# Sums of weight blocks and gated products on GpSimd, and another listing of the merged blocks, in a one-core encoder layer

## The chip, the cores and the metric

The kernel runs on 1 core of one Trainium2 chip. The metric is device time in microseconds (us) of one execution; of the kernel before, 3 runs gave 1290.79 to 1299.38 us with a median of 1297.6 us. One further execution was profiled: it took 1294.25 us. The core has five instruction queues that are named here as the profile names them: PE (TensorE, matmuls; PEld is its weight load), DVE (VectorE), ACT (ScalarE), POOL (GpSimd) and SP (SyncE, here a queue for DMAs). Each queue runs in order, and an instruction at its head waits on semaphores for what it needs.

## The reference

One layer on 512 tokens of width 2048, in float32. The three branches (forgetting attention, chunked attention with a relative bias, stick-breaking attention) have 4 heads of 128 each.

```python
hn = rmsnorm(x, norm_g)
proj = jnp.einsum('bsd,dc->bsc', hn, w_in)            # 2048 -> 12292 columns
br = proj[..., :QKVG_COLS].reshape(b, s, 3, 4, 512)   # q, k, v, gate path of each branch
f_logit = proj[..., QKVG_COLS:QKVG_COLS + N_HEADS] + b_f
gates = jax.nn.sigmoid(proj[..., QKVG_COLS + N_HEADS:] + b_gate).reshape(b, s, 3, 2048)
ya = forgetting_attention(qa, ka, va, f_logit)        # qa, ka, qb, kb are normalised first
yb = chunked_relpos_attention(qb, kb, vb)
yc = stick_breaking_attention(qc, kc, vc)
ys = jnp.stack([ya, yb, yc], axis=2) * jax.nn.silu(br[:, :, :, 3])
up = jnp.einsum('bsnw,nwd->bsnd', ys, w_up)           # 512 -> 2048 in each branch
merged = jnp.sum(gates * up, axis=2)
return x + jnp.einsum('bsd,de->bse', merged, w_out)
```

## The kernel before

**Products of three matmuls.** A float32 product is made from parts that PE multiplies at its faster rate. A block of weights, 128x1024, is loaded into a tile `raw`; ACT writes its rounded part to `wh` (L409), DVE the rest, `wl = raw - wh` (L419), both in `prep`. PE then multiplies the high part of the activations by `wh`, the low part by `wh` and the high part by `wl` (L277). One block of weights is a *unit* of the program; PE works through 405 units in a fixed order. There are 2 buffers for `wl` and 3 for `wh` (`LA = 2`), so that the `wl` of a unit can be written from the end of the unit two before it.

**Strassen tasks.** The input projection of two column groups, and the output projection in two halves, are 2x2 block products with 7 products in place of 8 (`Strassen`, `Product`): 11 tasks for the input and 2 for the output, of 28 units each. A unit of a task is product p of chunk c, with 12 matmuls; the order is p = 5, 1, 6, 7, 2, 3, 4 with c = 0 to 3 in each (`PLAIN`; the first output task has another order). Products 1, 2, 4 load a block, product 5 loads one and has a second added to it by a DMA of the POOL queue that accumulates (`add_up`, L320). The weights of products 6 and 3 are sums in place: `sum_up` adds the block of (1, c) to that of (5, c), which makes the weights of (6, c), and later the block of (2, c) to that, which makes those of (3, c). These 104 sums are the DVE instruction L630. After the first of the two, the block of (1, c) gets another accumulating DMA and becomes the weights of (7, c). There are 8 `raw` buffers.

**The end of the program.** After the input tasks come 24 units of the up projection in four groups g of 512 columns, three branches b each (`up_units`, order in `UPS`). For each block of 128 tokens, DVE multiplies the product by its gate (L1321) and, for b = 1 and 2, adds it to the sum of the branches (L1328, 32 instructions). The merged blocks must be turned before the output projection, which is done in two ways. Groups in `DRAMS` (0, 2 and 1) are turned in 32x32 squares by DVE (L1354, `folded`), stored, and read back with their squares in new places by four SP DMAs a block (L312, `back`, called by `turned_m`). Group 3 is turned by PE (L1385, `spun_m`), and ACT copies the result from PSUM (L1392). A turned block is tile `m`, and `arrived` lets the sums begin that make the operands of the output projection: `merged_a` (groups 0 and 1, first DVE step L1401) and `merged_b` (groups 2 and 3). On PE the input tasks, the up units and the output tasks follow one another without a break in the program.

**What sets the order.** A planner in Python (`Flow`) runs through all steps before the program is written. A step is a generator that yields what it waits for, and an engine with an estimated cost; of the steps that could go first on an engine, the one with the earliest start is written next, and of equals the one with the earliest due time, which is its ready time and its slack. The planner's times decide the order in each queue and nothing else; on the chip the queues run on semaphores. `turned_m` waits in the planner's time for the estimated landing and `MEXTRA` more; but `arrived` then lets `merged_a` or `merged_b` begin from `flow.fin`, the end of the instruction written last, and not from that landing:

```python
        ev = yield from back(m, md[g][:, :, blk(i)])
        yield Event(ev.t + MEXTRA)
        arrived(g, i, m)
...
            spawn(merged_a(k, m), 4.0, flow.fin)
```

Of the kernel before, what the change touches and what calls it, by code (L numbers as in the profile page):

```python
# [16 lines left out]
S = 512  # L17
# [8 lines left out]
UK = 8  # L26
# [11 lines left out]
PE, ACT, DVE, SP, POOL = 0, 1, 2, 3, 4  # L38
# [26 lines left out]
class Flow:  # L65
# [16 lines left out]
    def give(self, slots, n=1):  # L82
        slots.free += [self.fin] * n

    def spawn(self, gen, slack, ready=None):
        task = Task(gen, slack, self.now if ready is None else ready)
        self.tasks.append(task)
        self.advance(task)
# [81 lines left out]

def dve_us(n, x=1):
    return x * (0.1 + 0.00105 * n)


@with_exitstack
def hybrid_kernel(
# [12 lines left out]
    nc = tc.nc  # L189
# [17 lines left out]
    flow = Flow()  # L207
    spawn, set_, give = flow.spawn, flow.set, flow.give
# [3 lines left out]
    def t2(s, dt=F32):  # L212
        return tp.tile([P, S], dt, tag="t2", name=nm(s))
# [13 lines left out]
    def blk(i):  # L227
        return slice(i * P, (i + 1) * P)
# [3 lines left out]
    def two(ap):  # L232

        return ap.rearrange("p (h s) -> p h s", h=2)
# [20 lines left out]
    def split(hi, lo, src, n, ev=None, due=(), hi_ev=None):  # L255

        yield (ACT, act_us(n), *due)
        nc.scalar.activation(hi, src, AF.Copy)
        if hi_ev is not None:
            set_(hi_ev)  # L260
        yield (DVE, dve_us(n), *due)
        nc.vector.tensor_sub(lo, src, f(hi))  # L262
        if ev is not None:
            set_(ev)

    def minus(to, a, b):

        nc.vector.scalar_tensor_tensor(to, a, -1.0, b, op0=ALU.mult, op1=ALU.subtract)
# [38 lines left out]
    def back(to, src):  # L307

        n = src.shape[0] * 4
        for b in range(4):  # L310
            yield issue(0.54)
            nc.sync.dma_start(to[32 * b:32 * (b + 1), :].rearrange("p (n c) -> p n c", c=32),  # L312
                              src.rearrange("t (a r) c -> (t a) r c", r=32)[:, :, 32 * b:32 * (b + 1)]
                              .rearrange("n r c -> r n c"))
            ev = Event(landing(flow.fin, n * 4, 128) + PIECES)
        return ev
# [60 lines left out]
    def at(u, g, slack=5.0):  # L377
        side.setdefault(u, []).append((g, slack))
# [44 lines left out]
    def products(u, ps, kts, tbs, block, first=False, last=False, bank=None, done=None, outer=False, gate=None,  # L423
                 more=False):

        for group in [[tb] for tb in tbs] if outer else [tbs]:
            if bank is not None:
                for tb in group:
                    yield bank[0], 1
                    ps[tb] = bank[1]()  # L430
            if gate is not None:
                for tb in group:
                    yield gate(tb)
            for j, kt in enumerate(kts):
                for tb in group:
                    yield lambda: block(kt, tb) is not None
                    h, lo, ev = block(kt, tb)
                    yield ev
                    yield PE, mm_us(S, 2)
                    mm(ps[tb], h, u.hi[:, j, :], first and j == 0, more=more)  # L440
                    mm(ps[tb], lo, u.hi[:, j, :], more=more)
            yield u.ready
            for j, kt in enumerate(kts):
                for tb in group:
                    yield PE, mm_us(S)
                    mm(ps[tb], block(kt, tb)[0], u.lo[:, j, :], stop=last and j == len(kts) - 1, more=more)
            if last:
                for tb in group:
                    spawn(done(tb), 1.0, flow.fin)
# [142 lines left out]
    class Product(Unit):  # L592
# [31 lines left out]
        def sum_up(self):  # L624
            task, c = self.task, self.c
            own, after = (5, 6) if self.p == 1 else (6, 3)
            to = task.unit(own, c)
            yield to.ready
            yield DVE, dve_us(2 * S)
            nc.vector.tensor_add(to.raw, to.raw, self.raw)  # L630
            set_(task.unit(after, c).there)
            if self.p == 2:
                give(raws)
                return
            u = task.unit(7, c)
            u.raw = self.raw
            yield from self.more(Event(flow.fin), u)
# [670 lines left out]
    merged, merged_ev = {}, {}  # L1308

    def up_units(g, b):  # L1310
        n = (C, B, A)[b]
        ps = [None] * QB
        for tb in range(QB):
            sig_ev[n, g, tb] = Event()
            merged_ev[b, g, tb] = Event()

        def taken(tb):
            yield sig_ev[n, g, tb]
            t = sig[n, g, tb]
            yield DVE, dve_us(S)  # L1320
            nc.vector.tensor_mul(t, ps[tb], t)  # L1321
            give(accs)
            if b == 0:
                merged[g, tb] = t
            else:
                yield merged_ev[b - 1, g, tb]
                yield DVE, dve_us(S)
                nc.vector.tensor_add(merged[g, tb], merged[g, tb], t)  # L1328
                give(t2s)
            set_(merged_ev[b, g, tb])  # L1330

        def mms(i):
            def block(k, tb):
                y = b * NH + 2 * i + k
                return ys[y] and (*ys[y].block(tb), y_ev[y])

            def go(u):
                yield from products(u, ps, (0, 1), range(QB), block, i == 0, i == 1, None if i else (accs, acc),
                                    done=taken, outer=True)
            return go  # L1340

        return [Unit(mms(i), srcs=[w_up[g, b, i]]) for i in range(2)]
# [7 lines left out]
    def folded(g, tb):  # L1350
        yield merged_ev[NB - 1, g, tb]
        m = merged[g, tb]
        yield DVE, dve_us(S) + 0.07
        nc.vector.transpose(m, m)  # L1354
        if g not in md:
            md[g] = dp.tile([QB, P, S], F32, name=nm("md"))
        md_ev[g, tb].t = (yield from store(md[g][tb], m, 256, t2s)).t + LATER
# [3 lines left out]
    def turned_m(g, i):  # L1361
        for tb in range(QB):
            yield md_ev[g, tb]
        yield t2s, 1
        m = t2("m")
# [4 lines that stand above are left out]
    def arrived(g, i, m):  # L1370
        k = 4 * g + i
        if k < UK:
            kept_m[k] = m
            spawn(merged_a(k, m), 4.0, flow.fin)
        else:
            spawn(merged_b(k - UK, m), 3.0, flow.fin)

    def spun_m(g, i):
        for tb in range(QB):
# [18 lines left out]
    def merged_a(k, a):  # L1398

        yield DVE, dve_us(HS)  # L1400
        nc.vector.tensor_sub(a[:, RH], a[:, LH], a[:, RH])  # L1401
        yield xps, 1
        m1[k] = Parts("m1", [m1_ev[k]] * 2)
        yield from split(m1[k].hi, m1[k].lo, two(a), S, m1_ev[k])

    def merged_b(k, b):
        a = kept_m[k]
        yield m1_ev[k]
        yield t2s, 1
        t = t2("mt")  # L1410
        if k % 2 == 0:
            yield t2s, 1
            mus[k // 2] = t2("mu")
        u = mus[k // 2][:, RH if k % 2 else LH]
        q = DVE, dve_us(HS)
        yield q
        minus(t[:, LH], b[:, RH], a[:, RH])
        yield q
        minus(t[:, RH], t[:, LH], a[:, LH])
        give(t2s)  # L1420
        yield q
        minus(u, t[:, LH], b[:, LH])
        yield xps, 1
        ev = Event()
        m23[k] = Parts("m23", [ev, ev])
        yield from split(m23[k].hi, m23[k].lo, two(t), S, ev)
        give(t2s)
        if k % 2 == 0:
            yield xps, 1
            m4[k // 2] = Parts("m4")  # L1430
            set_(m4_ev[k // 2])
        yield xps, 1
        ev = Event()
        m2[k] = Parts("m2", [ev, ev])
        yield from split(m2[k].hi, m2[k].lo, two(b), S, ev)
        give(t2s)
        yield m4_ev[k // 2]
        h, lo, ev = m4[k // 2].half(k % 2)
        yield from split(h, lo, u, HS, ev)
        if k % 2:  # L1440
            give(t2s)

    for g, b in UPS:
# [5 lines left out]
        for i in range(QB):  # L1449
            if g in DRAMS:  # L1450
                at(len(units) - 1, lambda g=g, i=i: folded(g, i))
# [100 lines left out]
NR = 8  # L1552

UPS = [(0, 0), (0, 1), (2, 0), (2, 1), (0, 2), (2, 2)] + [(g, b) for g in (1, 3) for b in range(3)]
DRAMS = (0, 2, 1)
MLATE, MSKIP = 2.5, 1

EARLY = 0.5
# [4 lines left out]
HSLACK = 12.0  # L1563
ENDSLACK, ENDOFF = 3.0, 3
EARLYG = 1
MEXTRA = 8.0

_OUT = (QB, NQ, P, S)

# [45 lines left out]
```

## Time and profile before

| | |
|---|---|
| runs | 1290.79, 1297.6, 1299.38 us |
| profiled execution | 1294.25 us, of which the span from the first to the last instruction is 1292.5 us |
| granted TensorE clock, mean | 0.996 |
| busy share of the span: PE, PEld | 99%, 81% |
| DVE, ACT, POOL | 77%, 58%, 7% |
| DMA | 286.51 MB, mean 222 GB/s |

"Busy" is read for each engine by itself: the PE row is an upper figure, since matmuls overlap and their ends are modelled. A row of the time line gives start, duration, engine, line of the code, operation, output <- inputs, shape, number of instructions merged in the row, and in square brackets the idle time before it with what ended that. A row of groups has the number of instructions, their busy time, the mean of one in ns, and the idle time before them. Line numbers are those of the kernel before; those of the kernel after are 4 higher from L175 to the end of the planned program.

### The profile page before, as it was taken

Reading aid. Unit: us, or ns where it says so; the run is one execution under the profiler, and the core shown is the slowest. Engines: PE = TensorE matmul, PEld = TensorE weight load, DVE = VectorE, ACT = ScalarE, POOL = GpSimd, SP = SyncE. Lnnn points to the kernel's source line nnn. Section 1 sums busy time; section 2 is a strip of 40 time slices with the busy share of each in tenths; the row PEclk is TensorE's granted clock in tenths of the full one; section 3 lists DMA queues with packets and bytes.
Section 4 is the critical chain, followed back from the end, with each engine's and each line's share of the span. In section 5 each row is a group of like instructions: output and inputs, shape, how many; then the busy total and the mean of one; then the engine's idle time right before and its main releaser. Section 6 shows DMA issues by size and latency. Waiting matters only on the chain. (4 is left out here: it accounts for less than half of the span.)

```text
span 1292.5 us, 17358 instructions
## 1 busy us (share of the span) xinstructions
PE 1274.2 (99%) x5700; PEld 1050.2 (81%) x5700; DVE 999.5 (77%) x1402; ACT 752.2 (58%) x1239; POOL 91.7 (7%) x115
## 2 busy tenths in 40 slices
PE   9999999999999999999999999999999998989998
PEld 7788888888888888888888788887887786868887
DVE  6948896978969677686876878868788686898665
ACT  7836565645756567565575665755656532564442
POOL 0001010110101101011010110101100000010100
PEclk9999999999999999999999999999999999989999
DMA  9685899987889878897889978889889979946963
GB/s 356 207 206 123 216 235 215 265 200 209 222 201 281 191 218 228 199 272 196 222 223 208 271 183 220 230 192 287 189 217 342 286 228 211 265 94 224 238 169 129
DMA packets 269690, 286.51 MB, mean 222 GB/s; under 512 B 178320, under 2 KB 189072, under 8 KB 269600
## 3 DMA queue, kind: packets, MB, share of 16 engines
q1 hardware_dynamic: 252176, 226.42, 59.0%
q0 software_dynamic: 14976, 54.53, 22.6%
q10 hardware_dynamic: 2448, 4.46, 0.9%
q8 instruction: 45, 0.74, 0.2%
q14 instruction: 45, 0.37, 0.1%
HBM read 241.78 MB, written 43.56 MB: 221 GB/s over the span
## 5 line engine op out<-in xcount | busy, mean ns | idle before, releaser
L419 DVE TENSOR_TENSOR wl<-raw,wh 128x1024 fp32r<-128x1024 f32 (+1 forms) x405 | 492.5, 1217 | 215.5 <-PE acc L277 138.7
L409 ACT ACTIVATE wh<-raw 128x1024 fp32r<-128x1024 f32 (+1 forms) x404 | 426.0, 1056 | 359.8 <-PE acc L277 327.9
L277 PE MATMUL acc<-wh,x 128*128 128x512 f32 x1664 | 424.0, 390 | 0.1
L277 PEld LDWEIGHTS acc<-wh,x 128*128 128x128 f32 x1664 | 312.0, 188 | 68.4 <-issue 3.4
L277 PE MATMUL acc<-wh,t 128*128 128x512 f32 x1056 | 275.4, 390 | 2.4 <-ACT wh L409 2.4
L277 PEld LDWEIGHTS acc<-wh,t 128*128 128x128 f32 x1056 | 197.3, 188 | 43.2 <-ACT wh L409 3.3
L277 PE MATMUL acc<-wl,x 128*128 128x512 f32 x832 | 232.2, 389 | 0.1
L277 PEld LDWEIGHTS acc<-wl,x 128*128 128x128 f32 x832 | 155.8, 188 | 32.5 <-DVE wl L419 0.5
L277 PE MATMUL acc<-wl,t 128*128 128x512 f32 x528 | 154.6, 391 | 0.2
L320 POOL DMA_DIRECT2D raw<-in_w_col x88 | 76.1, 865 | 846.4 <-DMA raw<-in_w_col 136.7
L630 DVE TENSOR_TENSOR raw<-raw,raw 128x1024 f32<-128x1024 f32 x104 | 126.7, 1218 | 0.1
L277 PEld LDWEIGHTS acc<-wl,t 128*128 128x128 f32 x528 | 98.2, 188 | 21.5 <-DVE wl L419 2.0
L277 PE MATMUL acc<-wh,m 128*128 128x512 f32 x448 | 114.4, 389 | 0.0
L277 PE MATMUL acc<-wh,y 128*128 128x512 f32 x384 | 104.2, 393 | 0.0
L277 PEld LDWEIGHTS acc<-wh,m 128*128 128x128 f32 x448 | 84.0, 188 | 17.5
L277 PEld LDWEIGHTS acc<-wh,y 128*128 128x128 f32 x384 | 72.6, 189 | 15.1
L277 PE MATMUL acc<-wl,m 128*128 128x512 f32 x224 | 64.7, 395 | 5.7 <-DVE wl L419 5.7
L277 PE MATMUL acc<-wl,y 128*128 128x512 f32 x192 | 60.4, 394 | 4.2 <-DVE wl L419 4.2
L714 ACT ACTIVATE u<-acc 128x512 f32<-128x512 f32 x52 | 31.1, 599 | 41.4 <-PE acc L277 41.3
L277 PEld LDWEIGHTS acc<-wl,m 128*128 128x128 f32 x224 | 42.3, 190 | 15.1 <-DVE wl L419 6.5
L277 PEld LDWEIGHTS acc<-wl,y 128*128 128x128 f32 x192 | 36.4, 191 | 12.7 <-DVE wl L419 5.3
L1321 DVE TENSOR_TENSOR sg<-acc,sg 128x512 f32<-128x512 f32 x48 | 32.6, 685 | 7.2 <-ACT sg L1305 3.6
(155 smaller groups left out, 951.3 us busy)
## 6 DMA issues: line engine op xcount, KB each, us to landing
raw<-in_w_col SPq DMA_DIRECT2D x191, 512.0 KB, 5.0
raw<-in_w_col POOLq DMA_DIRECT2D x88, 512.0 KB, 8.2
raw<-in_w_out SPq DMA_DIRECT2D x32, 512.0 KB, 4.8
raw<-in_w_up SPq DMA_DIRECT2D x24, 512.0 KB, 4.9
sg<-gl SPq DMA_DIRECT2D x48, 256.0 KB, 5.2
gl<-u SPq DMA_DIRECT2D x44, 256.0 KB, 4.8
raw<-in_w_out POOLq DMA_DIRECT2D x16, 512.0 KB, 6.8
qkl<-qd SPq DMA_DIRECT2D x96, 64.0 KB, 4.0
```

Of the source, the lines that this page charges most:

```text
L277: nc.tensor.matmul(ps, w, x, start=start, stop=stop, skip_group_check=more)
L320: nc.gpsimd.dma_start(to, src, accum_op=ALU.add)
L409: nc.scalar.activation(u.hi, u.raw, AF.Copy)
L419: nc.vector.tensor_sub(u.lo, u.raw, f(u.hi))
L630: nc.vector.tensor_add(to.raw, to.raw, self.raw)
L714: nc.scalar.activation(t, w, AF.Copy)
L1321: nc.vector.tensor_mul(t, ps[tb], t)
```

## The change

There are three edits. The 104 sums of weight blocks and the 32 sums of gated products become GpSimd instructions, on the POOL queue, with a cost of 0.2 + 0.0022 n us in the planner. The steps on turned blocks are listed from the estimated landing (`flow.ready` at that point is the landing with `MEXTRA`), `MEXTRA` is 4.0 and not 8.0, and the slack of `merged_a` is 1.0 and not 4.0; that of `merged_b` stays 3.0. Group 1 leaves `DRAMS`, so that PE turns it as it does group 3.

```diff
+def pool_us(n, x=1):
+    return x * (0.2 + 0.0022 * n)
...
             to = task.unit(own, c)
             yield to.ready
-            yield DVE, dve_us(2 * S)
-            nc.vector.tensor_add(to.raw, to.raw, self.raw)
+            yield POOL, pool_us(2 * S)
+            nc.gpsimd.tensor_add(to.raw, to.raw, self.raw)
             set_(task.unit(after, c).there)
...
                 yield merged_ev[b - 1, g, tb]
-                yield DVE, dve_us(S)
-                nc.vector.tensor_add(merged[g, tb], merged[g, tb], t)
+                yield POOL, pool_us(S)
+                nc.gpsimd.tensor_add(merged[g, tb], merged[g, tb], t)
                 give(t2s)
...
         if k < UK:
             kept_m[k] = m
-            spawn(merged_a(k, m), 4.0, flow.fin)
+            spawn(merged_a(k, m), MAS, max(flow.ready, flow.fin))
         else:
-            spawn(merged_b(k - UK, m), 3.0, flow.fin)
+            spawn(merged_b(k - UK, m), MBS, max(flow.ready, flow.fin))
...
-DRAMS = (0, 2, 1)
+DRAMS = (0, 2)
...
-MEXTRA = 8.0
+MEXTRA = 4.0
+MAS = 1.0
+MBS = 3.0
```

Since the planner has other costs, nearly every queue has another order; PE runs the same matmuls in the same order of units, with the attention products at other places between them. Three places are shown.

The DVE queue at products 1 of the fifth input task, before; `wl_3980` is that of unit (1, 0), `wl_4001`, `wl_4029` and `wl_4052` are those of (1, 1) to (1, 3), `wl_4078` is that of (6, 0):

```order
L419 TENSOR_TENSOR wl_3980<-raw_3800,wh_3955 128x1024
L630 TENSOR_TENSOR raw_3666<-raw_3666,raw_3800 128x1024
L902 STREAM_TRANSPOSE w_3912<-w_3912 128x384
L419 TENSOR_TENSOR wl_4001<-raw_3837,wh_3979 128x1024
L630 TENSOR_TENSOR raw_3694<-raw_3694,raw_3837 128x1024
L419 TENSOR_TENSOR wl_4029<-raw_3857,wh_3998 128x1024
L630 TENSOR_TENSOR raw_3720<-raw_3720,raw_3857 128x1024
L902 STREAM_TRANSPOSE v_3463<-v_3463 128x384
L419 TENSOR_TENSOR wl_4052<-raw_3882,wh_4028 128x1024
L630 TENSOR_TENSOR raw_3765<-raw_3765,raw_3882 128x1024
L419 TENSOR_TENSOR wl_4078<-raw_3666,wh_4051 128x1024
```

The same units on the DVE queue of the kernel after:

```order
L423 TENSOR_TENSOR wl_3975<-raw_3803,wh_3955 128x1024
L906 STREAM_TRANSPOSE w_3899<-w_3899 128x384
L423 TENSOR_TENSOR wl_4006<-raw_3834,wh_3974 128x1024
L906 STREAM_TRANSPOSE w_3912<-w_3912 128x384
L423 TENSOR_TENSOR wl_4030<-raw_3855,wh_4003 128x1024
L906 STREAM_TRANSPOSE v_3469<-v_3469 128x384
L423 TENSOR_TENSOR wl_4054<-raw_3883,wh_4029 128x1024
L423 TENSOR_TENSOR wl_4078<-raw_3663,wh_4053 128x1024
```

And its POOL queue there, where the sums now stand among the accumulating DMAs:

```order
L634 TENSOR_TENSOR raw_3663<-raw_3663,raw_3803 128x1024
L634 TENSOR_TENSOR raw_3690<-raw_3690,raw_3834 128x1024
L324 DMA raw_3803<-in_w_col 128x1024
L324 DMA raw_3834<-in_w_col 128x1024
L634 TENSOR_TENSOR raw_3719<-raw_3719,raw_3855 128x1024
L634 TENSOR_TENSOR raw_3776<-raw_3776,raw_3883 128x1024
L324 DMA raw_3855<-in_w_col 128x1024
L324 DMA raw_3883<-in_w_col 128x1024
```

The sums have left DVE; each accumulating DMA stands behind the sum of its block, and the third and fourth sums stand behind two of the DMAs.

The DVE queue of the kernel before at the first turned blocks; `m_9567` to `m_9569` are blocks of group 0 that a DMA brings back, and `wl_9627` is that of the 16th of the 24 up units:

```order
L1321 TENSOR_TENSOR sg_9443<-acc_9562,sg_9443 128x512
L419 TENSOR_TENSOR wl_9627<-raw_9275,wh_9577 128x1024
L1401 TENSOR_TENSOR m_9567<-m_9567 128x256
L1401 TENSOR_TENSOR m_9568<-m_9568 128x256
L1401 TENSOR_TENSOR m_9569<-m_9569 128x256
L262 TENSOR_TENSOR m_1681_9665<-m_9567,m_1681_9665 128x2x256
L419 TENSOR_TENSOR wl_9681<-raw_9311,wh_9625 128x1024
```

The same steps in the kernel after, where `wl_9727` is that of the 18th up unit:

```order
L423 TENSOR_TENSOR wl_9630<-raw_9282,wh_9581 128x1024
L423 TENSOR_TENSOR wl_9677<-raw_9315,wh_9628 128x1024
L1325 TENSOR_TENSOR sg_9483<-acc_9629,sg_9483 128x512
L1325 TENSOR_TENSOR sg_9484<-acc_9645,sg_9484 128x512
L1325 TENSOR_TENSOR sg_9530<-acc_9656,sg_9530 128x512
L1325 TENSOR_TENSOR sg_9531<-acc_9665,sg_9531 128x512
L423 TENSOR_TENSOR wl_9727<-raw_9367,wh_9676 128x1024
L1405 TENSOR_TENSOR m_9558<-m_9558 128x256
L1405 TENSOR_TENSOR m_9559<-m_9559 128x256
L1405 TENSOR_TENSOR m_9560<-m_9560 128x256
```

The steps on the first turned blocks have moved two units down the queue, behind the `wl` of the 18th up unit instead of the 16th.

The PE queue of the kernel after inside the 19th up unit; `sg_9390` to `sg_9445` are the merged blocks of group 1, whose last part was multiplied in the 18th:

```order
L281 MATMUL acc_9850<-wl_9779,y_8426 128x512
L1389 MATMUL att_9866<-identf,sg_9390 128x128
L1389 MATMUL att_9866<-identf,sg_9417 128x128
L1389 MATMUL att_9866<-identf,sg_9437 128x128
L1389 MATMUL att_9866<-identf,sg_9445 128x128
L1389 MATMUL att_9875<-identf,sg_9390 128x128
L1389 MATMUL att_9875<-identf,sg_9417 128x128
```

These 16 transposes are new on PE; they wait for the sums that GpSimd now makes, and the transposes of group 3 do so too, at the second unit of the output projection.

## The prediction

> **What bounds the kernel now.** The page of the profile comes first, then the waits of PE.
>
> ```profile
> span 1292.5 us, 17358 instructions
> PE 1274.2 (99%) x5700; PEld 1050.2 (81%) x5700; DVE 999.5 (77%) x1402; ACT 752.2 (58%) x1239; POOL 91.7 (7%) x115
> PE acc L277 <- DVE wl L419: 9.9, 3, 5.7
> PE acc L277 <- ACT wh L409: 2.4, 2, 1.5
> ```
>
> PE is the bound: it does matmuls nearly all the time, and DVE, busy for 77%, matters only where PE waits for a `wl`. It does so three times, 9.9 us in all, and the time line has the three places, with what DVE did there:
>
> ```profile
> 1076.48 1.07 PE L277 MATMUL acc<-wh,y 128*128 128x512 f32 x4
> 1077.68 1.43 DVE L1401 TENSOR_TENSOR m<-m 128x256 f32<-128x256 f32 x3 [10.05 <-DMA m<-md]
> 1079.62 1.22 DVE L419 TENSOR_TENSOR wl<-raw,wh 128x1024 fp32r<-128x1024 f32 x1
> 1080.89 0.73 PE L277 MATMUL acc<-wl,y 128*128 128x512 f32 x2 [3.34 <-DVE wl L419]
> 1089.10 0.73 PE L277 MATMUL acc<-wl,y 128*128 128x512 f32 x2 [0.83 <-DVE wl L419]
> 1132.27 0.43 DVE L1401 TENSOR_TENSOR m<-m 128x256 f32<-128x256 f32 x1 [6.25 <-DMA m<-md]
> 1136.82 2.08 PE L277 MATMUL acc<-wl,m 128*128 128x512 f32 x4 [5.71 <-DVE wl L419]
> ```
>
> All three are one fault of order: the steps on turned blocks stand in the DVE queue before their data has come back, so that DVE stands still for 10.05 and 6.25 us with a `wl` queued behind. Two stages of the time line and two rows of the chain of waits give the price with the slower clock that follows each pause:
>
> ```profile
> 1076.00:1090.00 14.00, 9.83 (x35) 7.27 (x34) 12.14 (x19) 7.86 (x12) 0.86 (x1) 0.88 0.80 153
> 1129.00:1143.00 14.00, 8.29 (x39) 6.70 (x37) 10.70 (x16) 5.84 (x9) 0.00 (x0) 0.76 0.37 69
> 1142.30 0.88 PE att L1385 x8
> 1143.18 145.43 PE acc L277 x640
> ```
>
> An undisturbed matmul takes 145.43 / 640 = 0.227 us, eight transposes 0.88 us. The first stage has 35 matmuls, 7.9 us of its 14.0; the second 23 and 16 transposes, 5.2 + 1.8 = 7.0 of 14.0. So 6.1 + 7.0 = 13.1 us are lost there, at a granted clock of 0.88 and 0.76.
>
> **The change part by part.**
>
> *The listing and the third group* take that cause away. The steps on group 0 now stand two up units further down the queue (24 matmuls each, 5.45 us at 0.227), 10.9 us, against a wait of 10.05 us. The blocks of group 1, for which DVE waited 6.25 us, come from PE and ACT and no DMA. I take all 13.1 us as gained. PE pays 16 transposes more, 2 x 0.88 = 1.8 us; the 16 DMAs and 4 DVE transposes that go were hidden. Sum: -11.3 us. Bounds: nothing gained and 1.8 lost, if the blocks land 5 us later than before, and -13.1.
>
> *The sums of gated products.*
>
> ```profile
> L1328 DVE TENSOR_TENSOR sg<-sg,sg 128x512 f32<-128x512 f32 x32 | 22.0, 690 | 0.7
> L630 DVE TENSOR_TENSOR raw<-raw,raw 128x1024 f32<-128x1024 f32 x104 | 126.7, 1218 | 0.1
> ```
>
> DVE is rid of 22.0 us that lay beside 130 us of PE work: nothing by itself. A sum on GpSimd is longer, but each has a whole up unit (5.45 us for four) until it is needed, except before the transposes, which are a rival below.
>
> *The sums of weight blocks* decide. DVE gets 126.7 us back, which is worth nothing while PE is the bound. What they can cost is time of DVE's `wl`. No row has a GpSimd sum; the nearest are three selects at the start, one beside a DVE instruction with two inputs in SBUF:
>
> ```profile
> 1.26 0.28 POOL L351 TENSOR_SCALAR_AFFINE_SELECT identf<-tmpc 128x128 f32<-128x128 f32 x1
> 1.50 0.28 POOL L354 TENSOR_SCALAR_AFFINE_SELECT mskc<-tmpc 128x128 f32<-128x128 f32 x1
> 5.02 0.74 DVE L491 SCALAR_TENSOR_TENSOR x<-x,small_in,x 128x512 fp32r<-128x512 f32 x1
> 5.22 0.70 POOL L468 TENSOR_SCALAR_AFFINE_SELECT mskf<-tmpc 128x128 f32<-128x128 f32 x1 [3.44 <-PE att L467]
> 6.11 0.75 DVE L491 SCALAR_TENSOR_TENSOR x<-x,small_in,x 128x512 fp32r<-128x512 f32 x1 [0.34 <-ACT x L486]
> ```
>
> For the price of a sum: 128 elements in 0.28 us make 8 x 0.28 = 2.24 us for 1024. That is one input. With two it could be twice that, 4.5 us; the lower bound is DVE's own 1.22. I take 2.25. For who waits: the third select took 0.70 and ended at 5.92, 0.16 after the DVE instruction, which took 0.74, no longer than the next of its kind, 0.75. So GpSimd was held up by DVE's two-input instruction. Whether a GpSimd instruction that is first holds up DVE, no row shows; I take it that it does, for its whole length.
>
> The Trainium skill says so ("SBUF — State Buffer", Who interferes with whom): a DVE instruction with two SBUF inputs and a GpSimd instruction that reads SBUF exclude each other, the first one keeping the shared port until it ends; here the trace agrees for DVE first. By the selects alone, DVE would lose nothing and the sum would end at -11.3 us; by the rule it pays what follows.
>
> The units at which it happens, in the fifth input task, DVE and PE:
>
> ```profile
> 432.31 1.22 DVE L419 TENSOR_TENSOR wl<-raw,wh 128x1024 fp32r<-128x1024 f32 x1
> 433.45 1.22 DVE L630 TENSOR_TENSOR raw<-raw,raw 128x1024 f32<-128x1024 f32 x1
> 435.03 1.23 DVE L419 TENSOR_TENSOR wl<-raw,wh 128x1024 fp32r<-128x1024 f32 x1 [0.36 <-issue]
> 437.80 1.19 DVE L419 TENSOR_TENSOR wl<-raw,wh 128x1024 fp32r<-128x1024 f32 x1
> 440.47 1.23 DVE L419 TENSOR_TENSOR wl<-raw,wh 128x1024 fp32r<-128x1024 f32 x1 [0.34 <-issue]
> 439.31 1.07 PE L277 MATMUL acc<-wl,x 128*128 128x512 f32 x4
> 441.12 0.62 PE L277 MATMUL acc<-wl,x 128*128 128x512 f32 x2
> 443.84 0.62 PE L277 MATMUL acc<-wl,t 128*128 128x512 f32 x2
> L320 POOL DMA_DIRECT2D raw<-in_w_col x88 | 76.1, 865 | 846.4 <-DMA raw<-in_w_col 136.7 <-DVE u L1162 126.0 <-DVE w L902 109.7
> ```
>
> The `wl` of (1, 1) starts at 432.31, those of (1, 2), (1, 3) and (6, 0) at 435.03, 437.80 and 440.47; PE uses the last three at 439.31, 441.12 and 443.84. A `wl` that starts on time so has 3.05, 2.13 and 2.14 us to spare. GpSimd's first two sums need nothing of these units and run before; the next two stand behind two DMAs, of which the second must wait until the `wl` of (1, 1) has read its block, at 433.53, and takes 0.87. The third sum runs from 434.4 to 436.7, and the `wl` due at 435.03 waits until then and ends at 437.9. If DVE and GpSimd take turns, the fourth sum then runs to 440.2, and the `wl` of (1, 3) to 441.4, where PE wants it at 441.1: 0.3 us of pause. If GpSimd does both sums in a row, to 438.9, the first `wl` ends at 440.1 for 439.31: 0.8 us. I take 0.6.
>
> At products 2 the blocks come from SP:
>
> ```profile
> 452.60 8.48 SPq L293 DMA_DIRECT2D raw<-in_w_col  x4
> ```
>
> Three steps in 8.48 us less one issue: they come at the pace of PE's units, 12 x 0.227 = 2.72 us, since a buffer comes free with each. Each turn of a sum and a `wl` is 2.25 + 1.22 = 3.47. After four turns DVE is up to 4 x 0.75 = 3.0 us late, or 0.9 beyond the 2.13 of the shortest unit, and where attention products lie between, as here, it is not late at all. I take 0.5.
>
> Behind the sums on POOL stand the accumulating DMAs, and behind those of products 2 the buffers that SP loads for products 4:
>
> ```profile
> raw<-in_w_col SPq DMA_DIRECT2D x191, 512.0 KB, 5.0
> raw<-in_w_col POOLq DMA_DIRECT2D x88, 512.0 KB, 8.2
> ```
>
> Both are hidden by units: (7, c) comes 8 units, 21.8 us, after (1, c), against 2.25 + 8.2; (4, c) 8 units after (2, c), against 2.25 + 5.0. A sum that is held up for 10 us would end that cover.
>
> So 1.1 us a task, for 11 input tasks and both output tasks (whose first takes its products 1 in pairs, so count 1.5): 12.5 x 1.1 = 13.8 us. A sum's 0.1 us more is 0.2 to 0.4 us in each of the two places, about 7 us in all.
>
> PE's other waits, 2.4 us for a `wh`, lie in input tasks where the planner has moved attention products and DMAs; I leave them as they are. **Sum**: 1294.25 - 11.3 + 13.8 = 1296.8 for an execution like the profiled one, which lay 3.35 below the median of the runs, 1297.6. So 1300 us, and 1292 to 1311 with a pause of 0.5 to 2.0 us a task.
>
> **The rivals.**
>
> *GpSimd never holds up DVE.* For it: the selects show only the reverse, and the sums have time (4 units of 2.72 us between (1, c) and (6, c)), so that a GpSimd that always gives way is early enough. Against it: a port that one side can hold is more simply held by either. Then 1297.6 - 11.3 = 1286 us, and 1283 if those 2.4 us go as well.
>
> *The sums are longer, and PE waits twice a task.* The mechanism is the one above, at the same units. With 2.6 us a sum, the third runs from 434.4 to 437.0 and the fourth at once to 439.6; the `wl` of (1, 2) ends at 440.8 for 439.31, 1.5 us; at products 2 four turns of 3.82 leave 4.4 late, 2.3 beyond. That is 3.8 a task, 47 us, and a net of +36: 1333 us; with turns taken, 0.9 at the first place and half of the 2.3 at the second, 2.1 a task, 26 us and 1312. It is over 1% slower from (13 + 11.3) / 12.5 = 1.9 us a task on, at sums of about 2.4 us. For it: two inputs are read where the select reads one. Against it: a fixed part of the 0.28 us, which does not grow.
>
> The Trainium skill gives 4497 ns for a GpSimd sum of 2048 float32 elements ("GPSIMD Engine Reference", Performance versus the Vector engine); half of that, 2.25 us, is an estimate by that page, and the sum by it is the 1300 above. No run here has shown it.
>
> *PE's transposes wait for GpSimd.* Those of group 3 stand 2.72 us behind the last up matmul: a DVE product, 0.69, and a sum, half of 2.25, leave 0.9 us for two hand-overs. If a `wl` of 1.22 comes between, PE pauses for under a microsecond at two places: 1302 us. If the order at the end does not heal, 11 us come back on top: 1313.
>
> **How the numbers follow.** Forecast, turns taken at about 2.25 us a sum: 0.38, of which little is above 1%. DVE never held up: 0.32, a quarter of it below -1%. Longer sums: 0.24, nearly all slower by over 1%. The end: 0.06, half of it slower. Faster by over 1% (under 1284.6; a run differs from the next by up to 0.7%, so 1% is about what can be told): 0.08. Slower by over 1% (over 1310.6): 0.22 + 0.03 + 0.03 of the forecast's edge = 0.28. Within: 0.64. The range reaches from the first rival to the middle of the second: 1283 to 1326. The likeliest time is 1300.
>
> **What would show it.** The groups of the profile after would have the sums on POOL at 2.2 to 2.3 us (a mean near 3 means that they wait for DVE), and the `wl` group with a mean well above 1217 ns if DVE is held up, 1217 if not; the waits would have PE waiting for `wl` at (1, 2), (1, 3), (6, 0) and at (3, 0) of most tasks, some 25 places. No DVE wait for `m<-md` over 2 us, and a clock near 1.0 between 1057 and 1143 us, would show the gain. A `wl` mean of 1217 with pauses of PE elsewhere would make the mechanism wrong; PE waiting for `wh` at (6, c) would say that GpSimd, not DVE, is late.

## The result and the profile after

The change made the kernel slower. Four runs gave 1399.1 to 1407.48 us with a median of 1403.65, beside 1294.19 for the kernel before on the same chip: a ratio of 1.0852, with a 95% interval of 1.0822 to 1.0882. The prediction said 1300 us, with a range up to 1326, and gave "slower by over 1%" a chance of 0.28. Direction and size were both missed.

The page of the profile after, with its first lines, the groups of the instructions in question, and PE's share of the waits; the last row is the group of `wl` in the profile before:

```profile
span 1400.2 us, 17458 instructions
PE 1314.3 (94%) x5716; PEld 1065.3 (76%) x5716; DVE 1060.1 (76%) x1262; ACT 755.4 (54%) x1243; POOL 429.2 (31%) x251
L423 DVE TENSOR_TENSOR wl<-raw,wh 128x1024 fp32r<-128x1024 f32 (+1 forms) x405 | 619.8, 1535 | 258.8 <-PE acc L281 180.7
L634 POOL TENSOR_TENSOR raw<-raw,raw 128x1024 f32<-128x1024 f32 x104 | 293.0, 2852 | 317.0 <-DMA raw<-in_w_col 231.4
L1332 POOL TENSOR_TENSOR sg<-sg,sg 128x512 f32<-128x512 f32 x32 | 50.1, 1577 | 113.9 <-DVE sg L1325 110.9
...
PEld acc L281 <- DVE wl L423: 46.7, 39, 3.3
PE acc L281 <- DVE wl L423: 30.0, 25, 2.9
PE att L278 <- DVE qkl L926: 13.3, 6, 4.7
PE att L1117 <- DVE al L266: 13.3, 11, 3.3
...
L419 DVE TENSOR_TENSOR wl<-raw,wh 128x1024 fp32r<-128x1024 f32 (+1 forms) x405 | 492.5, 1217 | 215.5 <-PE acc L277 138.7
```

DVE has 140 instructions fewer than before, and its busy time has risen, from 999.5 to 1060.1 us: the 405 steps that write `wl` take 1535 ns in the mean, where they took 1217. PE, busy for 99% before, is busy for 94% and waits for `wl` and for two DVE steps of the attention, `qkl` and `al`.

The loss isn't at the end of the program. Two stages of the time line from 17 to 1080 us, after and then before. In the kernel after they hold the input projection; the kernel before is through with it at 986 us and does up units behind that (in each row the stretch, its length, busy time and count of PE, PEld, DVE, ACT and POOL, the granted clock, the DMA share and GB/s):

```profile
17.00:400.00 383.00, 363.13 (x1578) 292.93 (x1577) 308.61 (x395) 217.37 (x361) 103.27 (x60) 0.98 0.77 201
400.00:1080.00 680.00, 633.14 (x2742) 514.49 (x2741) 513.73 (x608) 387.24 (x678) 208.38 (x116) 0.98 0.80 204
```

```profile
17.00:400.00 383.00, 382.94 (x1723) 314.67 (x1722) 308.48 (x450) 235.87 (x386) 27.74 (x32) 1.00 0.83 218
400.00:1080.00 680.00, 674.28 (x3018) 557.84 (x3016) 517.06 (x726) 407.75 (x711) 48.35 (x56) 1.00 0.86 232
```

In the same 1063 us PE does 4320 matmuls where it did 4741. The 421 that are missing are 96 us at 0.227 us each. Worked out from the records of PE, the 11 input tasks took 887.8 us before and take 986.3 us after, so that 98.5 us of the loss lie in them.

What one sum does to DVE and PE shows at products 1 of the fourth input task. DVE, POOL and PE on the time line:

```profile
377.14 1.18 DVE L423 TENSOR_TENSOR wl<-raw,wh 128x1024 fp32r<-128x1024 f32 x1
378.56 0.58 DVE L906 STREAM_TRANSPOSE w<-w 128x384 f32<-128x384 f32 x1 [0.24 <-ACT w L891]
379.44 6.26 DVE L423 TENSOR_TENSOR wl<-raw,wh 128x1024 fp32r<-128x1024 f32 x1 [0.30 <-PE acc L281]
379.56 5.04 POOL L634 TENSOR_TENSOR raw<-raw,raw 128x1024 f32<-128x1024 f32 x2
386.57 4.12 DVE L423 TENSOR_TENSOR wl<-raw,wh 128x1024 fp32r<-128x1024 f32 x1
386.93 2.67 POOL L634 TENSOR_TENSOR raw<-raw,raw 128x1024 f32<-128x1024 f32 x1
381.96 1.98 PE L281 MATMUL acc<-wh,x 128*128 128x512 f32 x8
385.75 1.56 PE L281 MATMUL acc<-wl,x 128*128 128x512 f32 x4 [1.82 <-DVE wl L423]
387.11 3.27 PE L281 MATMUL acc<-wh,x 128*128 128x512 f32 x8
390.75 1.19 PE L281 MATMUL acc<-wl,x 128*128 128x512 f32 x4 [0.38 <-DVE wl L423]
```

The `wl` that starts at 379.44 does its 1.2 us of work only when both sums are through, at 384.60, and ends at 385.70. GpSimd takes two sums in a row while DVE stands there, and the `wl` had started 0.12 us before the first of them. PE pauses for 1.82 us, and the eight matmuls behind, 1.98 us at 381.96, take 3.27 at 387.11: a slow clock follows the pause (0.65 granted in the mean from 387 to 391 us, 1.00 from 380 to 384). At 386.57 the same happens again with one sum.

### The profile page after: what moved, and what is told of

Read it like the earlier page. It is cut to its first block, busy times and chain, and to the rows that moved or that the text cites. A ratio compares the mean times of both kernels' runs of the same rounds, so it can differ in the third digit from the quotient of the medians.

```text
span 1400.2 us, 17458 instructions
## 1 busy us (share of the span) xinstructions
PE 1314.3 (94%) x5716; PEld 1065.3 (76%) x5716; DVE 1060.1 (76%) x1262; ACT 755.4 (54%) x1243; POOL 429.2 (31%) x251
## 5 line engine op out<-in xcount | busy, mean ns | idle before, releaser
L423 DVE TENSOR_TENSOR wl<-raw,wh 128x1024 fp32r<-128x1024 f32 (+1 forms) x405 | 619.8, 1535 | 258.8 <-PE acc L281 180.7
L281 PE MATMUL acc<-wh,x 128*128 128x512 f32 x1664 | 431.1, 395 | 5.0 <-ACT wh L413 4.5
L634 POOL TENSOR_TENSOR raw<-raw,raw 128x1024 f32<-128x1024 f32 x104 | 293.0, 2852 | 317.0 <-DMA raw<-in_w_col 231.4
L281 PE MATMUL acc<-wh,t 128*128 128x512 f32 x1056 | 278.4, 393 | 2.8 <-ACT u L718 2.8
L281 PE MATMUL acc<-wl,x 128*128 128x512 f32 x832 | 238.4, 397 | 23.2 <-DVE wl L423 22.7
L281 PE MATMUL acc<-wl,t 128*128 128x512 f32 x528 | 157.6, 396 | 0.8 <-DVE wl L423 0.7
L1332 POOL TENSOR_TENSOR sg<-sg,sg 128x512 f32<-128x512 f32 x32 | 50.1, 1577 | 113.9 <-DVE sg L1325 110.9
```

Of the source, the lines that this page charges most:

```text
L281: nc.tensor.matmul(ps, w, x, start=start, stop=stop, skip_group_check=more)
L423: nc.vector.tensor_sub(u.lo, u.raw, f(u.hi))
L634: nc.gpsimd.tensor_add(to.raw, to.raw, self.raw)
L1332: nc.gpsimd.tensor_add(merged[g, tb], merged[g, tb], t)
```

## The experiments

Of each kernel I give the median, the median of the kernel before on the same chip, and the ratio with its 95% interval. The diffs are against the kernel after, if nothing else is said.

**Both kinds of sums back on VectorE.** What is left of the change is the new listing and the third group on TensorE.

```diff
-            yield POOL, pool_us(2 * S)
-            nc.gpsimd.tensor_add(to.raw, to.raw, self.raw)
+            yield DVE, dve_us(2 * S)
+            nc.vector.tensor_add(to.raw, to.raw, self.raw)
...
-                yield POOL, pool_us(S)
-                nc.gpsimd.tensor_add(merged[g, tb], merged[g, tb], t)
+                yield DVE, dve_us(S)
+                nc.vector.tensor_add(merged[g, tb], merged[g, tb], t)
```

> The kernel after with both kinds of sums back on VectorE: only the listing from the landing and the third group on PE are left of the change. Theory 1 (GpSimd's sums hold up VectorE through a port that both read SBUF by; all of the loss is theirs): the tail gain of the prediction, 11 us, is there, so about 1283 us where the kernel before has 1294, no wait of DVE for a turned block above 2 us. Theory 2 (the loss comes from the new listing, which moved attention products and the work at the end): most of the 108 us stays, over 1380 us.

1285.7 us against 1293.95, ratio 0.9943 (0.992 to 0.9966). This is faster than both kernels. The whole loss, 118 us, belongs to the two kinds of sums. Of PE's waits only these are over 1 us:

```profile
span 1282.9 us, 17347 instructions
...
PE acc L281 <- DVE sg L1325: 2.2, 1, 2.2
PE att L1389 <- ACT m L1396: 1.7, 2, 1.1
PE att L471 <- DVE mskf L345: 1.1, 1, 1.1
```

The three stalls for `wl` before (9.9 us) are gone, but for 0.7 us at two places; three smaller ones, 3.9 us, have come between 1101 and 1115 us: one for `sg` and two for `m`.

**Only the weight sums back on VectorE.**

```diff
-            yield POOL, pool_us(2 * S)
-            nc.gpsimd.tensor_add(to.raw, to.raw, self.raw)
+            yield DVE, dve_us(2 * S)
+            nc.vector.tensor_add(to.raw, to.raw, self.raw)
```

> The kernel after with the 104 sums of weight blocks back on VectorE; the 32 sums of gated products stay on GpSimd. Theory 1: input tasks take 80 to 82 us each again, as before (8 to 9 less than in the kernel after), and only the up units pay, some 5 us for PE's transposes that wait for GpSimd: 1285 to 1293 us. Theory 2: input tasks stay near 89 us and the time near 1390.

1290.1 us against 1293.95, ratio 0.9977 (0.9957 to 0.9997). So the sums of gated products cost 4.4 us beside the kernel with both kinds on VectorE. The intervals of the two ratios overlap a little; the waits bear the size out and name the place, PE's transposes:

```profile
PE att L1389 <- POOL sg L1332: 5.4, 4, 2.4
```

**Memsets in place of the weight sums.** Order and waits stay as they are, GpSimd is busy at the same places for about 1.9 us each time, and reads nothing.

```diff
-            nc.gpsimd.tensor_add(to.raw, to.raw, self.raw)
+            nc.gpsimd.memset(to.raw, 0.01)
+            nc.gpsimd.memset(to.raw, 0.01)
```

> The kernel after with each sum of weight blocks replaced by two writes of a constant over the same block on GpSimd: the same order in every queue, the same waits, GpSimd busy for about 2 us at the same places, but it reads nothing from SBUF. The weights of products 6 and 3 are therefore constants. Theory 1: DVE's wl is back at a mean of 1217 ns, no two-input DVE instruction is held, and the time falls to 1285 to 1300 us. Theory 2 (the order, and products waiting for a slower GpSimd): the same pauses, over 1370 us.

1291.23 us against 1293.95, ratio 0.9978 (0.9962 to 0.9994). 112 of the 118 us are gone. The source view gives minimum, median and maximum in ns:

```profile
L423 DVE TENSOR_TENSOR wl<-raw,wh x405: 681/1224/2315, 7.1 to 1282.2; 128x1024 fp32r<-128x1024 f32 x134, 128x512 fp32r<-128x512 f32 x1
L634 POOL MEMSET raw<- x104: 948/955/1649, 95.1 to 1240.0; 128x1024 f32 x104
```

No `wl` takes longer than 2.32 us, where one took 6.26. So the new order in the queues isn't the cause, and neither is what waits for GpSimd. Two memsets are shorter than a sum, which takes 2.39 us undisturbed; that length alone isn't it either is shown by the kernel with one input below. What is left is that DVE stands still while GpSimd reads two blocks and adds them.

**Each weight sum as two instructions of half the length**, so that DVE has a chance between the halves.

```diff
-            nc.gpsimd.tensor_add(to.raw, to.raw, self.raw)
+            for h in range(2):
+                nc.gpsimd.tensor_add(to.raw[:, h, :], to.raw[:, h, :], self.raw[:, h, :])
```

> The kernel after with each sum of weight blocks made in two GpSimd instructions of 512 columns. The work on the port is the same, but VectorE can get its turn after 1.2 us and not after 2.4. Theory 1 with turns taken instruction by instruction: the longest wl falls from 6.3 us to below 4, DVE loses about the same in total as long as GpSimd has more to do, but the lag at the units that matter is about half: 1340 to 1380 us. If GpSimd keeps the port for both of its instructions, nothing changes: about 1400 us. Theory 2: 1404 us or more.

1386.67 us against 1293.95, ratio 1.0712 (1.0679 to 1.0745): 17 us better than after, outside the 1340 to 1380 that taking turns would have given. By the trace DVE does get its turn after one half at most places, but another step of DVE then meets the second half: 143 steps are over 0.15 us longer than undisturbed, and lose 180 us in all, where in the kernel after 98 lose 198. And nine `wl` still wait for four halves in a row; the longest takes 6.51 us.

**The weight sums alone, in the kernel before.** The diff is against the kernel before.

```diff
-            yield DVE, dve_us(2 * S)
-            nc.vector.tensor_add(to.raw, to.raw, self.raw)
+            yield POOL, pool_us(2 * S)
+            nc.gpsimd.tensor_add(to.raw, to.raw, self.raw)
```

> The kernel before with nothing changed but the sums of weight blocks, which GpSimd makes. If the port is the whole cause, the loss is the one that after has over the same listing with the sums on VectorE, 1404 - 1286 = 118 us, less up to 20 us for places at the end that only the new listing has: 1294 + 98 to 118 = 1392 to 1412 us. If the loss needs the new listing of the end or the gated sums as well, well under 1390 us.

1403.16 us against 1292.17, ratio 1.086 (1.0828 to 1.0893). This one edit, 111 us, gives the time of the whole change; listing and gated sums together add nothing to it that could be told.

**VectorE's account charged for the sums in the planner**, which GpSimd makes all the same (gated sums on VectorE).

```diff
-            yield POOL, pool_us(2 * S)
+            yield DVE, pool_us(2 * S)
             nc.gpsimd.tensor_add(to.raw, to.raw, self.raw)
```

> As after with the gated sums on VectorE, but the planner charges the time of each weight sum to VectorE, though GpSimd makes it: it so leaves VectorE a gap of the sum's length and lists its other steps around that. Theory 'unplanned': VectorE has 23% of the span idle, 290 us, and the 104 sums take 249 us at 2.39 us; the loss comes because the planner doesn't know that VectorE stands still, and a plan that knows recovers most of it: 1295 to 1330 us. Theory 'port': GpSimd takes the port when it likes, two sums in a row, and short steps of the attention still lose a whole sum each, planned or not: 1360 to 1405 us.

1384.67 us against 1292.17, ratio 1.0722 (1.0694 to 1.075). That is 19 us better than after, of which gated sums on VectorE are worth some 4. The plan puts part of the attention products behind the input tasks, so that stages can't be compared; the groups can, and two rows of PE's waits show a price of the plan:

```profile
L423 DVE TENSOR_TENSOR wl<-raw,wh 128x1024 fp32r<-128x1024 f32 (+1 forms) x405 | 603.5, 1497 | 242.1 <-PE acc L281 141.5 <-issue 48.3 <-ACT wh L413 31.9
L634 POOL TENSOR_TENSOR raw<-raw,raw 128x1024 f32<-128x1024 f32 x104 | 288.0, 2782 | 320.9 <-DMA raw<-in_w_col 199.8 <-DVE wl L423 74.1 <-DMA raw<-in_w_out 16.7
...
PE acc L281 <- DVE sg L1325: 16.0, 4, 10.2
PE acc L281 <- ACT y L262: 10.9, 3, 5.0
```

PE's pauses for `al` and `qkl` fall from 29 us to some 8, but after has no such pauses for `sg` and `y`. What room in the plan is worth to DVE by itself this run therefore doesn't settle; it does show that such room doesn't take the loss away. A `wl` still takes 1497 ns in the mean. A sum starts when its block lands and the `wl` that reads it is done, and no room in a plan keeps it from the next `wl`.

**One input in place of two.** GpSimd adds a constant to the block.

```diff
-            nc.gpsimd.tensor_add(to.raw, to.raw, self.raw)
+            nc.gpsimd.tensor_scalar_add(to.raw, to.raw, 0.01)
```

> As after, but in place of each weight sum GpSimd adds the constant 0.01 to the same block, which reads one block where the sum reads two (the weights of products 6 and 3 are so those of other products plus a constant). If any GpSimd instruction that reads SBUF holds VectorE's two-input instructions, VectorE is held here too, each time for this instruction's length: at 1.2 to 2.4 us long, 1310 to 1380 us, with steps of wl well over 2 us. If only an instruction with two inputs does, as with the memsets: 1288 to 1296 us, wl at 1.22.

1300.46 us against 1292.17, ratio 1.007 (1.005 to 1.0089): below the 1310 to 1380 of the one theory, above the 1288 to 1296 of the other. Groups of it, and the source view with minimum, median and maximum:

```profile
L423 DVE TENSOR_TENSOR wl<-raw,wh 128x1024 fp32r<-128x1024 f32 (+1 forms) x405 | 543.7, 1344 | 275.7 <-PE acc L281 181.1 <-issue 50.9 <-ACT wh L413 24.3
L634 POOL TENSOR_SCALAR raw<-raw x104: 2762/3113/12639, 94.6 to 1250.7; 128x1024 f32<-128x1024 f32 x104
```

The instruction is longer than the sum (2.76 us at the least, against 2.39), so by length it should have cost more. `wl` does lose time, 127 ns in the mean over all 405 where the sums cost 318: 60 `wl` are held, as many as in the kernel after, but for 0.8 us each and not 2.1. Most of that stays within what PE can cover (it waits 5.3 us for `wl` there, where after has 30.0), and beside the memsets the kernel loses 9 us (12 by the two ratios) and not 112. One input holds DVE for a shorter time than two; why, isn't settled by these runs.

**One kind of weight sum alone** on GpSimd, the gated sums on VectorE; in the first kernel those that products 1 make (`self.p == 1`), in the second those of products 2 (`self.p == 2`).

```diff
+            if self.p == 1:
                 yield POOL, pool_us(2 * S)
                 nc.gpsimd.tensor_add(to.raw, to.raw, self.raw)
+            else:
+                yield DVE, dve_us(2 * S)
+                nc.vector.tensor_add(to.raw, to.raw, self.raw)
```

> The listing of after with only the sums that products 1 make (into the blocks of products 5) on GpSimd; those of products 2 and the gated sums on VectorE. By the loss of after by products over 11 input tasks, products 5, 1 and 6 lose 43 us there, products 7 and 2 lose 56. If each kind of sum costs by itself where it runs: 1286 + 43 + about 5 in the output tasks = 1325 to 1345 us. If the loss comes mostly from later products that inherit the delay of these (the accumulating DMAs into the same blocks): above 1365. If it comes from the two kinds together: under 1310.

> The listing of after with only the sums that products 2 make (into the blocks of products 6) on GpSimd; those of products 1 and the gated sums on VectorE. The first kind alone cost 1333 - 1286 = 47 us, both 118. If the two kinds add up: 1286 + 71 = 1345 to 1365 us. If each adds to the other's delay (a block of products 6 late through the first kind is summed late by the second): under 1340 us.

The first: 1333.07 us against 1292.17, ratio 1.0324 (1.0301 to 1.0348), 47 us over the kernel with both kinds on VectorE. The second: 1327.17 against 1293.4, ratio 1.0267 (1.0237 to 1.0296), 41 us over it. Together they would be 89 us and measure 118, so 29 us come only with both kinds; the second lies in the range that was given for the case that each kind adds to the other's delay, under 1340. From the first matmul of a product's units to that of the next, summed over the 11 input tasks, in us, worked out from the traces:

```
                       p5     p1     p6     p7     p2     p3     p4
both on VectorE     123.2  120.4  119.7  139.2  119.7  141.2  121.1
sums of products 1  125.8  156.5  122.1  139.2  123.0  137.8  121.2
sums of products 2  128.0  121.3  130.8  145.2  150.0  130.9  119.7
the kernel after    132.2  160.2  128.6  173.7  143.0  127.6  120.9
```

Attention products lie among the units and move between the kernels. The same without the time of their own matmuls, at its undisturbed length:

```
                       p5     p1     p6     p7     p2     p3     p4
both on VectorE     120.1  119.8  119.7  120.3  119.7  120.4  121.1
sums of products 1  123.4  155.9  122.1  120.3  119.8  120.3  120.5
sums of products 2  124.9  119.9  120.2  137.6  140.1  120.1  119.7
the kernel after    130.3  155.1  121.7  160.5  135.5  120.1  119.7
```

The sums of products 1 cost 36 us at products 1, or 3.3 a task. The sums of products 2 cost 20 us at products 2, or 1.9 a task, and 17 at products 7, or 1.6 a task: 33 of their 44 in the input tasks begin while PE is still at products 7. With both kinds products 7 lose 40 us and not 17, so most of the 29 us lie there. More of the attention's matmuls stand there in the kernel after, 13.2 us of them for 7.6; that this is the reason fits, but no run isolates it. In the first, PE's pauses are for `wl` (30.2 us of 46.8 in the trace); in the second, for the attention's `al` and `qkl` (18.6 of 39.8) before `wl` (12.7).

**The listing alone**, with the third group turned through DRAM as before. The diff is against the kernel with both kinds of sums on VectorE.

```diff
-DRAMS = (0, 2)
+DRAMS = (0, 2, 1)
```

> As the kernel with both kinds of sums on VectorE (1285.7 us, ratio 0.994), but the third group's blocks are turned through DRAM again, as before, so that only the listing of the merged blocks' steps is new. If the gain at the end comes from the listing alone: PE's 16 transposes (1.8 us) and its two waits at them (2.0 us) go, 1282 to 1286 us. If the third group's turning by TensorE is what takes the 6.25 us wait away (the wait for its blocks comes back, as the prediction had it): 1289 to 1294 us.

1291.57 us against 1293.4, ratio 0.9983 (0.9963 to 1.0004), 5.9 us over the kernel with both edits (by the two ratios 5, give or take 4). The waits of PE, and the stage that had a clock of 0.76 before:

```profile
PE acc L281 <- DVE sg L1325: 3.3, 1, 3.3
PE acc L281 <- ACT m L262: 2.4, 1, 2.4
...
1129.00:1143.00 14.00, 11.34 (x52) 8.81 (x51) 11.34 (x18) 7.34 (x11) 1.73 (x2) 0.88 0.55 112
```

`wl` is late at one place only, for 1.0 us, but the blocks of group 1 still are late, and PE waits for an operand made from them, `m`. It takes TensorE's turning to remove that, and its 1.8 us are well spent.

## Why the prediction was wrong

**What bounds the kernel** was right, and so was the mechanism named for the weight sums: a sum on GpSimd keeps DVE's `wl` from running. The rival of longer sums even had the sign. The step that failed is the term "1.1 us a task", 13.8 us in all, and in it the count of where DVE is held and of who pays. Measured, the weight sums cost 111 us in the kernel before, and the input tasks of the kernel after lose 9.3 us each beside those with both kinds of sums on VectorE.

*Where.* The prediction let a sum collide with `wl` at two places a task, the units (1, 2) and (1, 3) and the end of products 2, for 0.6 and 0.5 us. In the trace DVE is held at 98 instructions, 198 us over their undisturbed times, of which 60 are `wl` with 128 us. In the kernels with one kind alone, products 1 lose 3.3 us a task for the 0.6, and the sums of products 2 cost 3.4 for the 0.5, nearly half of it at products 7, which the prediction didn't look at. Products 3, where it looked for the late `wl`, lose nothing.

*Turns.* I took 0.6 as the value between turns (0.3) and two sums in a row (0.8). Two in a row is what the records at 379.56 show, and there PE ran out of finished `wl`: it paused for 1.82 us, and for 0.38 at the next unit.

*Length.* The sum takes 2.39 us when nothing disturbs it, by the least of 104:

```profile
L634 POOL TENSOR_TENSOR raw<-raw,raw x104: 2390/2692/12277, 94.1 to 1364.5; 128x1024 f32<-128x1024 f32 x104
```

The estimate was 2.25, and the rival of longer sums set its point of 1.9 us a task at 2.4. Even that rival, which came nearest, ended at 1333 us: it kept the two places and `wl` as the only one to pay.

*Who pays.* The attention's steps on DVE were left out altogether; the prediction even held that "where attention products lie between", DVE "is not late at all". DVE, POOL and PE where the sums of products 2 run beside the attention:

```profile
411.08 3.32 DVE L423 TENSOR_TENSOR wl<-raw,wh 128x1024 fp32r<-128x1024 f32 x1 [1.50 <-PE acc L281]
414.32 8.18 DVE L266 TENSOR_TENSOR al<-al,ah 128x512 fp32r<-128x512 f32 x4
422.43 0.74 DVE L926 SCALAR_TENSOR_TENSOR qkl<-qkl,gq,qkh 128x512 fp32r<-128x512 f32 x1
410.92 11.10 POOL L634 TENSOR_TENSOR raw<-raw,raw 128x1024 f32<-128x1024 f32 x4 [17.23 <-DMA raw<-in_w_col]
417.20 0.80 PE L1117 MATMUL att<-al,vh 128*128 128x512 f32 x1 [3.27 <-DVE al L266]
422.36 0.39 PE L1117 MATMUL att<-al,vh 128*128 128x256 f32 x1 [0.84 <-DVE al L266]
598.57 0.47 PE L278 MATMUL att<-qkh,qkl 128*128 128x128 f32 x1 [4.67 <-DVE qkl L926]
```

Here the two engines do take turns, and that is the bad case: four `al`, of 0.7 us or less each by themselves, take 8.18 us: the first three wait for a sum each, and the `wl` at 411.08 for the one before. A short step pays as much as a long one. PE's attention product stands in its queue ahead of the matmuls of the units, which wait with it, 3.27 us here and 4.67 at 598.57. Pauses for `al` and `qkl` make 29.7 us of the 91.4 that PE stands still in this trace; those for `wl` 35.7.

*The clock.* The prediction costed pauses alone. Worked out from the records of PE, against the time of its matmuls undisturbed, 1260.3 us before and 1262.0 with the 16 transposes:

```
                 span    PE stands still   at places   the rest over undisturbed matmuls
before         1292.5          17.2            15             15.0
after          1400.2          91.4            74             46.8
two memsets    1291.2          16.4            19             12.8
```

A pause costs itself and nearly half of itself again: 74.2 us more of pauses came with 31.8 us more of slowed matmuls. (Where a pause is taken to end shifts a few us between these two columns.) The granted clock agrees: at 0.978 in the mean for 0.996 it lost some 26 us more. The prediction did read this in the profile of before, where 9.9 us of waits cost 13.1, and used it for the gain and not for the loss.

**The Trainium skill's rule** that was set against the selects ("SBUF — State Buffer", Who interferes with whom) decided rightly that DVE is held up: with the selects alone the forecast would have been 1286 us. Its "first one" holds for most steps, but not as a sure way to count: of the `wl`, `al` and `qkl` that met a sum, 64 of the 71 that started behind it were held, and 24 of the 33 that started ahead were not; the `wl` at 379.44 was recorded before the sum and ended after it.

**The listing and the third group** were right in mechanism and somewhat too large. The prediction had -11.3 us; the kernel without the sums has -8.3 (by its interval -10.4 to -4.4, which leaves the -11.3 outside). That is nearly all of the 9.9 us of waits and their slow clock gone, and new waits for `sg` and at the transposes, 3.9 us, that the prediction did not look for. The stage from 1057 to 1143 us, whose clock was to be near 1.0, has 0.98 in that kernel:

```profile
1057.00:1143.00 86.00, 82.09 (x369) 67.24 (x368) 70.47 (x114) 43.99 (x68) 5.18 (x6) 0.98 0.78 189
```

Of the split by cause, the third group's turning came near, 5.9 us for 5.2. The listing did not: it was to give 6.1 us, and alone it gives 1.8, with an interval that reaches zero.

**The sums of gated products** were costed at nothing; alone they cost 4.4 us. The rival for PE's transposes had the place (1302 for 1300, a chance of 0.06), as "under a microsecond at two places"; it measured 5.4 us at four. In the kernel after, these rows of POOL and PE show how:

```profile
1192.71 4.61 POOL L1332 TENSOR_TENSOR sg<-sg,sg 128x512 f32<-128x512 f32 x3
1194.57 0.33 PE L1389 MATMUL att<-identf,sg 128*128 128x128 f32 x1 [2.07 <-POOL sg L1332]
1195.97 0.47 PE L1389 MATMUL att<-identf,sg 128*128 128x128 f32 x1 [1.07 <-POOL sg L1332]
```

Three sums come one after the other, at 1.5 us each, where DVE took 0.69, and the transposes, which need a finished block each, wait for one after the other.

**What would show it** named the right rows: the `wl` mean rose, PE waits for `wl` at 25 places by the row of the waits (and its weight load at 39), and the sums' mean of 2852 ns is "near 3", which was to mean that they wait for DVE as well. One sum did so for long: it starts at 1247.55 and is the longest of the row above, 12277 ns, while DVE goes from one two-input step to the next without a gap until 1257.6 us. The places were right only in part: 14 of the 17 pauses for `wl` in the input tasks lie at (1, 1), (1, 2) and (1, 3), none at (6, 0) or (3, 0), and eight lie behind the input tasks.

**Open** is why the 29 us that appear only with both kinds of sums come, most of them at products 7, and why one input does so much less than two.

## What to carry to other kernels

Before a step goes to GpSimd to relieve a VectorE that isn't the bound, ask not only how long it takes there but what VectorE will be doing meanwhile: each step of VectorE with two inputs in SBUF that meets it, short ones too, can wait for the whole of it, as here for 2.4 us, and for the next one also. Count all of them, not those of the loop in question, and look at what stands behind each in the bounding engine's in-order queue. A stand-in that keeps the order and the waits but reads nothing tells such contention from a fault of order in one run; a second one, as long as the step it stands for, tells it from the length.

## What was not expected of the hardware

Which DVE instructions are held up could be counted in the trace of after: those whose undisturbed time would fall into a weight sum, and how many of them took over 0.15 us longer than the same form in the kernel with both kinds of sums on VectorE:

```
                                              met a sum   held   us lost
wl<-raw,wh          two inputs in SBUF            85        57    126.2
al<-al,ah           two inputs in SBUF            11         9     18.6
qkl<-qkl,gq,qkh     inputs in SBUF                 8         7     14.7
u<-u,xr             two inputs in SBUF             6         3      6.1
vl<-vl,vh           two inputs in SBUF             4         3      3.5
three forms of m    two inputs in SBUF            10         0      0.0
v<-acc,v            one input in PSUM             15         0      0.0
att<-att,mskf       one input in PSUM              8         0      0.0
STREAM_TRANSPOSE    one input                     10         0      0.0
```

Forms that met three sums or fewer, and steps on one column, are left out. Those with an input in PSUM were not held although 22 of the 23 started behind a sum's start. The ten `m` are another matter: all lie beside the one sum of 12.28 us, and there it was the sum that waited.

Two of those that were not held, beside a sum that ran from 508.41 to 511.45:

```profile
509.27 0.69 DVE L272 SCALAR_TENSOR_TENSOR v<-acc,v 128x512 f32<-128x512 f32 x1
510.62 0.69 DVE L272 SCALAR_TENSOR_TENSOR v<-acc,v 128x512 f32<-128x512 f32 x1 [0.67 <-PE acc L281]
508.41 3.04 POOL L634 TENSOR_TENSOR raw<-raw,raw 128x1024 f32<-128x1024 f32 x1 [5.22 <-DMA raw<-in_w_col]
```

The other things were these: a `wl` recorded 0.12 us ahead of a sum still came behind it; two sums in a row passed one waiting `wl` (6.26 us for 1.22), while elsewhere the two engines took turns; and an instruction with one input, of 2.76 us, cost the kernel 9 us over the memsets where the sum with two, of 2.39 us, cost 112.
